# A fourth pair's token sums and 96 of 256 row pairs in seven products, in a four-layer decoder trunk

## The chip, the cores and the metric

One core of a Trainium2 chip runs the whole program. The metric is the device time of one execution in microseconds, as the median of three runs. TensorE (PE) multiplies, VectorE (DVE) and ScalarE (ACT) prepare operands and take results, SyncE (SP) and ScalarE issue the loads.

## What is computed

The reference is a trunk of two rounds over 256 tokens of width 2048, all in 32-bit floats: a mixer (round 0: a recurrent head group and pooling; round 1: sparse attention), an MLP of width 8192 and a gated embedding add. The change is in the MLPs:

```
hn = rmsnorm(h, ln_mlp_g[i])
h = h + jnp.square(jax.nn.relu(hn @ mlp_w_up[i])) @ mlp_w_down[i]
```

`mlp_w_up` is 2048 x 8192 and `mlp_w_down` 8192 x 2048.

## The kernel before

Every product of 32-bit numbers is done as three matmuls of a faster format. A weight tile `raw` is split into `hi`, its rounding (L204, ScalarE), and `lo`, the rest (L211, VectorE); the activations are split in the same way. Then `product` (L706) runs x_hi * hi (L710), x_lo * hi (L711) and x_hi * lo (L712) into one bank of PSUM. The third of them is the first that needs `lo`.

An MLP is done in 16 sets (`mm_set`): for each quarter q of the inner width two up sets, Up(q,0) and Up(q,1), and then two down sets, Down(q,0) and Down(q,1). The second number (n2) is the half of the output columns. A set gives 256 tokens x 1024 columns, from 8 pairs of rows of 128 x 2. One pair is one load of 1 MB: two rows (k) by two columns of 512 (n). With the two token halves (t) that makes a product of 2x2 by 2x2 blocks.

- A *plain* pair takes eight products, in two steps of four products (`plain`).
- An *owned* pair takes seven products (`own_fns`), in four steps of 1, 2, 2 and 2 products. For that VectorE first forms sums of the weight blocks: `first` (L735, 128x1024) and `second` (L740 and L741, 128x512 each), and the products read kept sums of the tokens, `ph["S"]`. At the end of a set `out1` to `out3` (L757 to L770) put the additional banks together.

Which pairs of a set are owned, and in what order the pairs run, stands in the constants TWO (pairs 2 and 3) and THREE (1, 2 and 3). THREE is used for Up(q,0) with q > 0 and for Down(q,1) with q < 3, TWO for all others: 38 owned pairs of 128 in an MLP, 76 of 256 in both.

```
TWO, THREE = ((2, 3), (0, 1, 4, 5, 2, 6, 3, 7)), ((1, 2, 3), (0, 4, 1, 5, 2, 6, 3, 7))
```

The token sums of the pairs 1, 2 and 3 are formed in `x_after` (`keep`, `sums`) for the MLP's input, in the sets of the mixer's out projection, and in `up_out` (`sums`, `s_back`, `s_split`) for the inner values. There each pair's sums are turned by four transposes (L963).

The order on each engine is written out by hand. `run` goes through the steps. Ahead of a step's matmuls it issues the weight sums of the step four later (SUMS) and the `hi` of the step two later (LOOK), behind them the work that `after` has put at this step, and then the `lo` of the step two later. The tile pools hold four `hi`, four `lo` and three `raw` buffers, and the weight sums use three slots. The results of a set are worked up in the first steps of the next: after a down set `adds` (L838, VectorE) and `wide` (L831), after an up set `adds` (L932), the relu and its square (ScalarE), transposes (L808) and splits (L946, L950).

The mixers' small tiles (`ttile`, 12 of 128 x 256) live in the pool `sm`, which is open for the whole program.

Of the kernel before, what the change touches and what calls it, by code (L numbers as in the profile page):

```python
# [14 lines left out]
P = 128  # L15
# [97 lines left out]
def trunk(ctx: ExitStack, tc: tile.TileContext, a: dict, out: bass.AP):  # L113
# [18 lines left out]

    def utile():
        return sm.tile([P, 4, T], F32, name="u", bufs=1)

    def ttile():
        return sm.tile([P, T], F32, name="t", bufs=12)
# [285 lines left out]
    lp = l0.enter_context(tc.tile_pool(name="lp", bufs=1))  # L423
    invc = lp.tile([P, 4, 16], F32, name="invc")
# [242 lines left out]
    def tools():  # L667

        mp = ph["mp"] = ExitStack()
        pool_ = mp.enter_context(tc.tile_pool(name="mp", bufs=1))  # L670
        m = big(F32, (P, 8, 512))
        ph["T"] = [m[:, 2 * i:2 * i + 2, :] for i in range(3)]
        ph["nT"] = 0
        ph["w2"] = m[:, 6:8, :]
        S = big()
        one = pool_.tile([P, 2, 4, T], F32R, name="s1")
        ph["S"] = []
        for i in range(2):
            two = S[:, 4 * i:4 * i + 4, :].rearrange("p a n -> p (a n)").rearrange("p (i s n) -> p i s n", i=2, s=4)
            ph["S"].append({1: one[:, i], 2: two[:, 0], 3: two[:, 1], (2, 3): two, (1,): one[:, i:i + 1]})  # L680
        ph["pT"] = pool_.tile([P, 2, 512], F32R, name="pT")
# [137 lines left out]
    TWO, THREE = ((2, 3), (0, 1, 4, 5, 2, 6, 3, 7)), ((1, 2, 3), (0, 4, 1, 5, 2, 6, 3, 7))  # L819
# [34 lines left out]
    def x_after(n2, banks, X, gi, sx=None, at=0):  # L854
# [22 lines left out]
        def keep(which):  # L877
            fx = box["fx"] = box.get("fx") or wtiles()
            for x, i in enumerate(which):
                for j in range(2):  # L880
                    act.activation(fx[len(which) - 1][:, x, j * T:(j + 1) * T], scratch(banks, i)[:, j], AF.Copy,
                                   scale=gain(2 * i + j))

        def sums(which):
            fx = box["fx"][len(which) - 1][:, :len(which)].rearrange("p i (j t) -> p i j t", t=T)
            f = s_sums(len(which), *(fx[:, :, j, t * P:(t + 1) * P] for t in range(2) for j in range(2)))
            S = ph["S"][sx][which]
            act.activation(S[:, :, :, :P], f, AF.Copy)
            after(1, lambda: dve.tensor_tensor(S[:, :, :, P:], f, S[:, :, :, :P].bitcast(F32), op=OP.subtract))
# [7 lines left out]
        if sx is not None and n2 == 0:  # L897
            after(at + 1, lambda: keep((1,)))
            after(at + 2, lambda: keep((2, 3)))
            after(at + 4, lambda: sums((1,)))  # L900
            after(at + 6, lambda: sums((2, 3)))
# [19 lines left out]
    def mlp(l, X, Xn):  # L921
# [3 lines left out]
        def up_out(q, n2):  # L925
            def post(w, banks):
# [26 lines left out]
                def sums(which):  # L953
                    v = [W[t][:, len(which) - 1].rearrange("p (i j c) -> p i j c", j=2, c=P)[:, 2 - len(which):] for t in range(2)]
                    f = s_sums(len(which), v[0][:, :, 0], v[0][:, :, 1], v[1][:, :, 0], v[1][:, :, 1])
                    for x, i in enumerate(which):
                        after(1, lambda x=x, i=i: s_back(i, f[:, x]))
                        after(2, lambda i=i: s_split(i))
# [17 lines left out]
                if n2 == 0:  # L976
                    after(3, lambda: sums((1,)))
                    after(4, lambda: sums((2, 3)))
# [9 lines left out]
        for q in range(4):  # L988
            for n2 in range(2):
# [3 lines left out]
                own, order = THREE if q and n2 == 0 else TWO  # L993
                mm_set(lambda p, q=q, n2=n2: a["mlp_w_up"][l][q][n2][p], order, X, post, own, 0)
            for n2 in range(2):
                own, order = THREE if n2 and q < 3 else TWO
# [123 lines left out]
    def open1():  # L1120
        kp = l1.enter_context(tc.tile_pool(name="kp", bufs=1))
        at["kp"] = kp
# [325 lines left out]
```

## Time and profile before

| | us |
|---|---|
| median of three runs | 2294.92 (2294.54 to 2295.27) |
| the profiled run | 2295.85 |
| its span in the profile | 2293.8 |
| TensorE busy | 2269.0, 99% |
| VectorE busy | 1797.9, 78% |
| ScalarE busy | 1340.6, 58% |

The profile is of one execution. Busy times are those in which an engine has an instruction running; a matmul's record is longer than the time to the next matmul's start, since they run one into the other. The profile's names are those of the program: `big` is any of the large tiles (activations, kept sums, weight sums), `ps` a bank of PSUM.

### The profile page before, as it was taken

How to read it: one execution, taken by the hardware profiler on the slowest of the kernel's cores; microseconds unless marked ns; L12 is line 12 of the kernel's file. 1: busy time of each engine (PE TensorE's matmuls, PEld its weight loads, DVE VectorE, ACT ScalarE, POOL GpSimd, SP SyncE). 2: the span in 40 equal slices, each digit the busy share in tenths (PEclk: the TensorE clock that was granted, in tenths of full speed). 3: DMA queues.
4: the chain of work that ended last, by engine and by line, in shares of the span. 5: the costliest groups of instructions: out<-in, count | busy, mean ns of one | idle time of the engine just before them, and what ended most of it. 6: DMA issues, size and time to landing. Idle time of an engine off the chain costs nothing.

```text
span 2293.8 us, 30360 instructions
## 1 busy us (share of the span) xinstructions
PE 2269.0 (99%) x11506; PEld 1927.0 (84%) x11506; DVE 1797.9 (78%) x2475; ACT 1340.6 (58%) x1940; POOL 14.6 (1%) x42
## 2 busy tenths in 40 slices
PE   8999999999999999999999999999999999999997
PEld 8998888888888888889889988888888888888886
DVE  6786688988988987856875676688988988988865
ACT  6665565565566565665564454566566565565654
POOL 2000000000000000000000000000000000000000
PEclk9999999999999999999999999999999999999999
DMA  7645555555555555555775224555555555555553
GB/s 259 213 155 179 204 184 202 202 184 200 204 184 196 206 185 199 187 183 204 255 275 177 87 93 159 176 184 200 190 198 196 192 199 194 194 199 191 204 194 129
DMA packets 69539, 436.58 MB, mean 190 GB/s; under 512 B 9872, under 2 KB 14352, under 8 KB 18448
## 3 DMA queue, kind: packets, MB, share of 16 engines
q1 hardware_dynamic: 64832, 427.90, 54.0%
q10 hardware_dynamic: 4560, 6.74, 0.9%
q8 instruction: 90, 1.47, 0.3%
q14 instruction: 57, 0.47, 0.1%
HBM read 432.51 MB, written 2.10 MB: 189 GB/s over the span
## 4 chain that ended last, share of the span: by engine, by line
PE 97%; DVE 1%; DMA 0%; ACT 0%; issue 0%; SPq 0%; DVEq 0%; ACTq 0%
PE ps L712 25%; PE ps L710 25%; PE ps L711 25%; PE ps L295 11%; PE ps L299 3%; PE ps L808 2%; PE ps L1390 1%; PE ps L300 1%; PE ps L1180 1%; PE ps L963 0%; DVE lo L211 0%; DMA raw<-in_ab_w_in 0%; PE ps L1332 0%; PE ps L1330 0%; PE ps L1333 0%; PE ps L588 0%
## 5 line engine op out<-in xcount | busy, mean ns | idle before, releaser
L211 DVE TENSOR_TENSOR lo<-raw,hi 128x1024 fp32r<-128x1024 f32 (+1 forms) x817 | 935.9, 1158 | 159.1 <-ACT hi L204 158.4
L204 ACT ACTIVATE hi<-raw 128x1024 fp32r<-128x1024 f32 (+1 forms) x817 | 813.3, 1008 | 382.8 <-PE ps L711 300.5
L710 PE MATMUL ps<-hi,big 128*128 128x512 f32 x2436 | 954.5, 392 | 0.0
L712 PE MATMUL ps<-lo,big 128*128 128x512 f32 x2436 | 948.8, 389 | 0.0
L711 PE MATMUL ps<-hi,big 128*128 128x512 f32 x2436 | 948.1, 389 | 0.0
L712 PEld LDWEIGHTS ps<-lo,big 128*128 128x128 f32 x2436 | 457.2, 188 | 96.2 <-DVE lo L211 0.6
L711 PEld LDWEIGHTS ps<-hi,big 128*128 128x128 f32 x2436 | 457.5, 188 | 92.9
L710 PEld LDWEIGHTS ps<-hi,big 128*128 128x128 f32 x2436 | 457.4, 188 | 92.8
L204 ACT ACTIVATE hi<-big 128x1024 fp32r<-128x1024 f32 x152 | 161.4, 1062 | 253.3 <-PE ps L711 213.2
L295 PE MATMUL ps<-big,hi 128*128 128x256 f32 x1408 | 264.5, 289 | 7.7 <-ACT hi L204 7.7
L211 DVE TENSOR_TENSOR lo<-big,hi 128x1024 fp32r<-128x1024 f32 x152 | 185.8, 1222 | 90.8 <-ACT hi L204 90.8
L295 PEld LDWEIGHTS ps<-big,hi 128*128 128x128 f32 x1408 | 223.1, 193 | 9.7 <-ACT hi L204 7.7
L295 PE MATMUL ps<-big,lo 128*128 128x256 f32 x704 | 200.5, 285 | 1.0 <-DVE lo L211 0.9
L295 PEld LDWEIGHTS ps<-big,lo 128*128 128x128 f32 x704 | 135.8, 193 | 1.6 <-DVE lo L211 1.6
L299 PE MATMUL ps<-big,hi 128*128 128x512 f32 x320 | 113.6, 398 | 0.0
L735 DVE TENSOR_TENSOR big<-raw 128x1024 f32<-128x1024 f32 x76 | 92.6, 1219 | 0.4 <-DMA raw<-in_mlp_w_down 0.2
L300 PE MATMUL ps<-big,lo 128*128 128x256 f32 x320 | 89.7, 280 | 0.6 <-DVE lo L211 0.5
L299 PEld LDWEIGHTS ps<-big,hi 128*128 128x128 f32 x320 | 60.1, 188 | 14.1
L950 DVE TENSOR_TENSOR big<-ps,big 128x512 fp32r<-128x512 f32 x64 | 41.1, 684 | 36.6 <-ACT big L946 36.6
L300 PEld LDWEIGHTS ps<-big,lo 128*128 128x128 f32 x320 | 60.3, 189 | 2.0 <-DVE lo L211 1.5
L411 ACT ACTIVATE big<-ps,gains 128x256 fp32r<-128x256 f32 x80 | 31.2, 472 | 42.6 <-PE ps L808 42.6
L741 DVE TENSOR_TENSOR big<-big,raw 128x512 f32<-128x512 f32 x76 | 52.6, 692 | 2.6
(256 smaller groups left out, 1630.2 us busy)
## 6 DMA issues: line engine op xcount, KB each, us to landing
raw<-in_mlp_w_up SPq DMA_DIRECT2D x128, 1024.0 KB, 4.9
raw<-in_mlp_w_down SPq DMA_DIRECT2D x128, 1024.0 KB, 4.9
raw<-in_c_w_in SPq DMA_DIRECT2D x36, 1024.0 KB, 4.9
raw<-in_ple_w_gate SPq DMA_DIRECT2D x32, 1024.0 KB, 4.9
raw<-in_ab_w_in SPq DMA_DIRECT2D x20, 1024.0 KB, 4.9
raw<-in_ab_w_out SPq DMA_DIRECT2D x16, 1024.0 KB, 4.9
raw<-in_c_w_out SPq DMA_DIRECT2D x16, 1024.0 KB, 4.9
raw<-in_c_cmp_w_k SPq DMA_DIRECT2D x8, 1024.0 KB, 4.9
```

What stands on the lines that cost most here:

```text
L204: act.activation(halves[s]["hi"][:, k, :w], halves[s]["src"][:, k, :], AF.Copy)
L211: dve.tensor_tensor(lo[:, k, :w], src[:, k, :], halves[s]["hi"][:, k, :w].bitcast(F32), op=OP.subtract)
L295: pe.matmul(b, lhsT=wt[:, kk, cols], rhs=x[:, x0:x0 + T], start=first and n == 0 and j % 2 == 0, stop=last and n == 2, skip_group_check=True)
L299: pe.matmul(b, lhsT=hi[:, kk, cols], rhs=x, start=first, stop=False, skip_group_check=True)
L300: pe.matmul(b[:, T:], lhsT=lo[:, kk, cols], rhs=x[:, :T], start=False, stop=last, skip_group_check=True)
L710: pe.matmul(b, lhsT=x_hi, rhs=hi[:, n, :], start=r not in begun, stop=False, skip_group_check=True)
L711: pe.matmul(b, lhsT=x_lo, rhs=hi[:, n, :], start=False, stop=False, skip_group_check=True)
L712: pe.matmul(b, lhsT=x_hi, rhs=lo[:, n, :], start=False, stop=end, skip_group_check=True)
L735: dve.tensor_tensor(t, raw[:, 0::3, :], raw[:, 1:2, :].to_broadcast([P, 2, 512]), op=OP.add)
L741: dve.tensor_tensor(t[:, 1], t[:, 0], raw[:, 2], op=OP.add)
L808: pe.transpose(b[:, j, t * P:(t + 1) * P], of(t, i // 2, (2 * i + j) % 4), ident)
L950: dve.tensor_tensor(Hs[n2][:, k:k + 2, T:], scratch(banks, i), Hs[n2][:, k:k + 2, :T].bitcast(F32), op=OP.subtract)
```

## The change

Three constants say which pairs are owned and in which order. FOUR (pairs 0 to 3) is used for Up(q,0) with q > 0 and Down(q,1) with q < 3. THREE is used for all Up(q,1), where TWO stood. TWO stays for Up(0,0), for Down(q,0) and for Down(3,1). That makes 48 owned pairs an MLP, 96 of 256 in both. The order of THREE is another: the first owned pair runs one pair later, and in THREE and FOUR the pairs 2 and 3 follow one another.

For it the token sums of pair 0 are kept too: the tile `s1` doubles, `keep` copies pair 0 also, and `sums` forms the sums of 0 and 1 together where it formed those of 1 alone. To have space, `ttile` takes its tiles from a pool that lives only as long as a mixer.

```diff
     def ttile():
-        return sm.tile([P, T], F32, name="t", bufs=12)
+        return small["tp"].tile([P, T], F32, name="t", bufs=12)
...
-        one = pool_.tile([P, 2, 4, T], F32R, name="s1")
+        one = pool_.tile([P, 2, 2, 4, T], F32R, name="s1")
...
-            ph["S"].append({1: one[:, i], 2: two[:, 0], 3: two[:, 1], (2, 3): two, (1,): one[:, i:i + 1]})
+            ph["S"].append({0: one[:, i, 0], 1: one[:, i, 1], 2: two[:, 0], 3: two[:, 1], (0, 1): one[:, i], (2, 3): two})
...
-    TWO, THREE = ((2, 3), (0, 1, 4, 5, 2, 6, 3, 7)), ((1, 2, 3), (0, 4, 1, 5, 2, 6, 3, 7))
+    TWO, THREE, FOUR = (((2, 3), (0, 1, 4, 5, 2, 6, 3, 7)), ((1, 2, 3), (0, 4, 5, 1, 6, 2, 3, 7)),
+                        (range(4), (4, 0, 5, 1, 6, 2, 3, 7)))
...
-            after(at + 1, lambda: keep((1,)))
+            after(at + 1, lambda: keep((0, 1)))
             after(at + 2, lambda: keep((2, 3)))
-            after(at + 4, lambda: sums((1,)))
+            after(at + 4, lambda: sums((0, 1)))
             after(at + 6, lambda: sums((2, 3)))
...
                 if n2 == 0:
-                    after(3, lambda: sums((1,)))
+                    after(3, lambda: sums((0, 1)))
                     after(4, lambda: sums((2, 3)))
...
-                own, order = THREE if q and n2 == 0 else TWO
+                own, order = THREE if n2 else FOUR if q else TWO
...
-                own, order = THREE if n2 and q < 3 else TWO
+                own, order = FOUR if n2 and q < 3 else TWO
...
+        small["tp"] = l1.enter_context(tc.tile_pool(name="tp1", bufs=1))
```

In the changed kernel the lines lie two to five further down: `lo` is L213, `first` L738, `second` L743 and L744, `wide` L836, `adds` L843, the token sums L818, their split L974.

VectorE at the start of a set that follows a down set. Before, a set with three owned pairs, Up(q,0) or Down(q,1), from its second `lo` on (its first two pairs are 0 and 4, plain, then 1, owned):

```order
L211 TENSOR_TENSOR lo<-raw,hi 128x1024
L838 SCALAR_TENSOR_TENSOR h<-ps,rs,h 128x512 x2
L211 TENSOR_TENSOR lo<-raw,hi 128x1024 x2
L735 TENSOR_TENSOR big<-raw 128x1024
L211 TENSOR_TENSOR lo<-raw,hi 128x512
L740 TENSOR_TENSOR big<-big,raw 128x512
L741 TENSOR_TENSOR big<-big,raw 128x512
L831 SCALAR_TENSOR_TENSOR h<-u,rs,h 128x1024
L211 TENSOR_TENSOR lo<-raw,hi 128x1024
L211 TENSOR_TENSOR lo<-big,hi 128x1024 x2
L211 TENSOR_TENSOR lo<-raw,hi 128x1024
L831 SCALAR_TENSOR_TENSOR h<-big,rs,h 128x1024
```

The same place in the changed kernel, a set with four owned pairs (pair 4 plain, then 0, owned):

```order
L213 TENSOR_TENSOR lo<-raw,hi 128x1024
L738 TENSOR_TENSOR big<-raw 128x1024
L843 SCALAR_TENSOR_TENSOR h<-ps,rs,h 128x512 x2
L213 TENSOR_TENSOR lo<-raw,hi 128x512
L743 TENSOR_TENSOR big<-big,raw 128x512
L744 TENSOR_TENSOR big<-big,raw 128x512
L213 TENSOR_TENSOR lo<-raw,hi 128x1024
L213 TENSOR_TENSOR lo<-big,hi 128x1024
L836 SCALAR_TENSOR_TENSOR h<-u,rs,h 128x1024
L213 TENSOR_TENSOR lo<-big,hi 128x1024
L213 TENSOR_TENSOR lo<-raw,hi 128x1024 x2
```

The weight sums of the first owned pair have moved ahead of the second pair of `adds` and of the narrow `lo`, and the wide add stands between two `lo` of that owned pair.

VectorE at pairs 2 and 3 near the end of a set. In the changed kernel, from the sums for pair 2 to the last `lo` of pair 3:

```order
L738 TENSOR_TENSOR big<-raw 128x1024
L213 TENSOR_TENSOR lo<-raw,hi 128x512
L743 TENSOR_TENSOR big<-big,raw 128x512
L744 TENSOR_TENSOR big<-big,raw 128x512
L213 TENSOR_TENSOR lo<-raw,hi 128x1024
L213 TENSOR_TENSOR lo<-big,hi 128x1024 x2
L738 TENSOR_TENSOR big<-raw 128x1024
L213 TENSOR_TENSOR lo<-raw,hi 128x512
L743 TENSOR_TENSOR big<-big,raw 128x512
L744 TENSOR_TENSOR big<-big,raw 128x512
L213 TENSOR_TENSOR lo<-raw,hi 128x1024
L213 TENSOR_TENSOR lo<-big,hi 128x1024 x2
```

Before, the same place has the plain pair 6 between them, two `lo` more:

```order
L211 TENSOR_TENSOR lo<-big,hi 128x1024 x2
L211 TENSOR_TENSOR lo<-raw,hi 128x1024 x2
L735 TENSOR_TENSOR big<-raw 128x1024
L211 TENSOR_TENSOR lo<-raw,hi 128x512
L740 TENSOR_TENSOR big<-big,raw 128x512
```

What moved is the plain pair 6, from between the pairs 2 and 3 to ahead of pair 2.

VectorE in Up(q,1), in the middle of the work on Up(q,0), in the changed kernel, from the token sums of 0 and 1 on (L818, two groups of four), with the splits of the turned sums at L974:

```order
L818 TENSOR_TENSOR big<-u,big 128x2x128
L213 TENSOR_TENSOR lo<-raw,hi 128x1024
L738 TENSOR_TENSOR big<-raw 128x1024
L974 TENSOR_TENSOR s_2274<-ps,s_2274 128x4x128 x2
L213 TENSOR_TENSOR lo<-raw,hi 128x512
L743 TENSOR_TENSOR big<-big,raw 128x512
L744 TENSOR_TENSOR big<-big,raw 128x512
L974 TENSOR_TENSOR big<-ps,big 128x4x128 x2
L213 TENSOR_TENSOR lo<-raw,hi 128x1024
```

Before, no weight sums stood among these: the first owned pair came two steps later, and one split was fewer.

## Rows read from the trace of the kernel before

**Rows 1.** The page: busy time of the engines, and the chain that ended last
```profile
PE 2269.0 (99%) x11506; PEld 1927.0 (84%) x11506; DVE 1797.9 (78%) x2475; ACT 1340.6 (58%) x1940; POOL 14.6 (1%) x42
PE 97%; DVE 1%; DMA 0%; ACT 0%; issue 0%; SPq 0%; DVEq 0%; ACTq 0%
```
**Rows 2.** Stretches MLP 0, Down(0,1), Up(1,1): length; engines' busy; clock, DMA share, GB/s
```profile
253.40:948.00 694.60, 694.60 (x3168) 576.68 (x3167) 596.72 (x684) 416.22 (x522) 0.00 (x0) 1.00 0.57 194
386.63:428.22 41.59, 41.59 (x184) 34.35 (x183) 38.55 (x42) 23.06 (x25) 0.00 (x0) 1.00 0.59 203
469.82:515.16 45.34, 45.34 (x216) 37.79 (x214) 38.44 (x50) 28.76 (x39) 0.00 (x0) 1.00 0.54 186
```
**Rows 3.** Timeline of TensorE in Down(0,1): start, length, instruction
```profile
415.98 0.39 PE L710 MATMUL ps<-hi,big 128*128 128x512 f32 x1
...
421.42 0.39 PE L710 MATMUL ps<-hi,big 128*128 128x512 f32 x1
```
**Rows 4.** Timeline of VectorE in Down(0,1), from pair 3's sums to the end
```profile
412.36 1.22 DVE L735 TENSOR_TENSOR big<-raw 128x1024 f32<-128x1024 f32 x1
413.49 0.69 DVE L211 TENSOR_TENSOR lo<-raw,hi 128x512 fp32r<-128x512 f32 x1
414.09 0.68 DVE L740 TENSOR_TENSOR big<-big,raw 128x512 f32<-128x512 f32 x1
...
415.42 1.22 DVE L211 TENSOR_TENSOR lo<-raw,hi 128x1024 fp32r<-128x1024 f32 x1
416.56 1.22 DVE L211 TENSOR_TENSOR lo<-big,hi 128x1024 fp32r<-128x1024 f32 x1
419.14 1.23 DVE L211 TENSOR_TENSOR lo<-big,hi 128x1024 fp32r<-128x1024 f32 x1 [1.36 <-ACT hi L204]
...
422.98 1.22 DVE L211 TENSOR_TENSOR lo<-raw,hi 128x1024 fp32r<-128x1024 f32 x1
```
**Rows 5.** Timeline of VectorE at the start of Up(1,0), which begins at 428.22
```profile
428.57 1.22 DVE L211 TENSOR_TENSOR lo<-raw,hi 128x1024 fp32r<-128x1024 f32 x1
429.70 1.41 DVE L838 SCALAR_TENSOR_TENSOR h<-ps,rs,h 128x512 f32<-128x512 f32 x2
431.02 2.35 DVE L211 TENSOR_TENSOR lo<-raw,hi 128x1024 fp32r<-128x1024 f32 x2
...
436.36 1.28 DVE L831 SCALAR_TENSOR_TENSOR h<-u,rs,h 128x1024 f32<-128x1024 f32 x1
437.56 1.22 DVE L211 TENSOR_TENSOR lo<-raw,hi 128x1024 fp32r<-128x1024 f32 x1
```
**Rows 6.** Timeline of all engines in the out projection's second half: a wait of TensorE
```profile
219.80 1.23 DVE L211 TENSOR_TENSOR lo<-raw,hi 128x1024 fp32r<-128x1024 f32 x1
...
221.08 0.50 PE L712 MATMUL ps<-lo,big 128*128 128x512 f32 x1
...
221.41 0.39 PE L710 MATMUL ps<-hi,big 128*128 128x512 f32 x1
```
**Rows 7.** Timeline of VectorE in Up(1,1), which begins at 469.82: token sums
```profile
479.86 0.28 DVE L815 TENSOR_TENSOR big<-big 128x128 f32<-128x128 f32 x1
...
480.79 1.22 DVE L211 TENSOR_TENSOR lo<-raw,hi 128x1024 fp32r<-128x1024 f32 x1
481.93 0.42 DVE L815 TENSOR_TENSOR big<-big 128x256 f32<-128x256 f32 x1
...
483.39 1.22 DVE L211 TENSOR_TENSOR lo<-raw,hi 128x1024 fp32r<-128x1024 f32 x1
```
**Rows 8.** Timeline of TensorE in Up(1,1): four transposes between matmuls
```profile
482.26 0.39 PE L712 MATMUL ps<-lo,big 128*128 128x512 f32 x1
482.49 0.60 PE L963 MATMUL ps<-ident,big 128*128 128x128 f32 x4
...
483.16 0.40 PE L711 MATMUL ps<-hi,big 128*128 128x512 f32 x1
```
**Rows 9.** Timeline of ScalarE in the out projection's second half: copies of token tiles
```profile
217.23 1.59 ACT L881 ACTIVATE big<-ps,gains 128x256 f32<-128x256 f32 x4
```

## What was predicted

> **What bounds the kernel now.** I read the page first: TensorE is busy 99% of the span and the chain that ended last is 97% TensorE [rows 1]. Then the MLPs, where the change sits, by stretch: in the 694.6 us of MLP 0 TensorE is busy throughout at a granted clock of 1.00, VectorE 596.7 us, 86% [rows 2]. An average hides the sets, so I took two apart. Down(0,1), with three owned pairs, lasts 41.59 us and VectorE is busy for 38.55 of them, 93%. Up(1,1), with two owned pairs and more work after it, lasts 45.34 with VectorE busy for 38.44 [rows 2]. So the question is whether VectorE has room in the very sets that get more owned pairs.
>
> [...] What follows rests on the rows alone.
>
> TensorE's pace: 24 matmuls of 512 columns start between 415.98 and 421.42 [rows 3], 0.2267 us each. A plain pair is 24 of them, 5.44 us, in two steps of 2.72; an owned pair 21, 4.76 us, in steps of 3, 6, 6 and 6 (0.68 and three times 1.36).
>
> VectorE's pace, by starts since the records overlap by 0.08 [rows 4]: the sum of a whole load (`first`) 1.13, the two of `second` 1.33 together, a `lo` of two rows 1.14, of one row 0.60. An owned pair is 1.13 + 1.33 + 0.60 + 3 x 1.14 = 6.48 us of VectorE for 4.76 of TensorE; a plain pair 2 x 1.14 = 2.28 for 5.44. Owned pairs run VectorE into debt by 1.7 us, plain ones pay back. The lead with which a `lo` comes is bounded: at the end of a three-pair set the `lo` from 422.98 ends at 424.20 [rows 4], and its third matmul wants it at 425.50 + 0.45 = 425.95: 1.75 us ahead. Four `hi` and four `lo` buffers allow little more right after an owned pair: the `lo` at 419.14 waited 1.36 us for its `hi` [rows 4], which waited for a buffer that TensorE held.
>
> **Part by part.** *Products.* 20 more owned pairs save 3 matmuls each: 60 x 0.2267 = 13.6 us of TensorE.
>
> *Token sums of the pair 0.* After each of the 8 sets Up(q,0) four more transposes run: four of them stretch 0.45 us between the matmuls of 482.26 and 483.16 to 0.90 [rows 8], so 8 x 0.44 = 3.5 us back on TensorE. If only products and transposes counted, the change would gain 10.1.
>
> *VectorE per added owned pair*: 6.48 - 2.28 = 4.20 us more. Down(0,1) has 41.59 - 38.55 = 3.04 idle; with a fourth pair VectorE needs 38.55 + 4.20 = 42.75 where TensorE needs 41.59 - 0.68 = 40.91. The set can't be shorter than 42.75. That is the floor, with no idle VectorE left at all. There are 12 such sets (Down(q,1) for q 0 to 2, Up(q,0) for q 1 to 3, two layers).
>
> *Where a four-pair set stalls.* I follow VectorE in its new order from the set's start; it issues in order, and TensorE waits on the `lo` it needs at the third matmul of a step. The order 4, 0, 5, 1, 6, 2, 3, 7 makes pair 0 the steps 2 to 5, pair 1 the steps 8 to 11. In the trace the set at 428.22 has its second `lo` start at 428.57 [rows 5], 0.35 in; I take 0.42, as the set before ends with VectorE 0.08 later (below). The two adds of 128x512 take 1.32, a wide add 1.20 [rows 5].
> - Step 3 (second step of pair 0, wanted at 6.12 + 0.45 = 6.57): lo 1.14, `first` 1.13, adds 1.32, narrow lo 0.60, `second` 1.33, so the lo starts at 5.94 and with its record of 1.22 ends at 7.16. Late by 0.59.
> - Step 5 (wanted at 9.29): two lo 2.28 and the wide add 1.20, start 9.42, end 10.64. Late by 1.35 against the unstalled set.
> - Step 9 (pair 1, wanted at 16.77): three lo 3.42, `first`, narrow lo, `second`, wide add 4.26, start 17.10, end 18.32. Late by 1.55.
> - A wait costs more than its lateness: TensorE started 0.05 after the lo's end (221.03 to 221.08), and the next matmul 0.33 later instead of 0.23 [rows 6]; with slower ones behind it I take 0.15 to 0.2 a wait. So 1.7 by step 9.
> - Pairs 2 and 3 stand side by side, which no set of before has. Counted from a pair's start (418.02 in the rows, 15 matmuls before 421.42), its last lo ends at 2.35 (419.14 + 1.23 - 418.02), held back by the `hi` buffer as above; then `first` 1.13, narrow lo 0.60 and `second` 1.33 come before the lo of pair 3's second step, which starts at 5.33, ends at 6.55 and is wanted at 5.44 + 0.45 = 5.89. Late by 0.66, with the restart 0.85. Bounds for this unseen neighbourhood: nothing, if the earlier delay has given VectorE its time back, up to 1.36 more, if the wait for `hi` of [rows 4] comes once more.
> Sum: 40.80 + 1.7 + 0.85 = 43.35, against 41.59 before: +1.8 a set (floor +1.16). After pair 3 the lead recovers within pair 7 to the same 1.7 as before, 0.08 less. 12 x 1.8 = 21.6 us.
>
> *Up(q,1), 8 sets, two to three owned pairs.* TensorE: 0.68 less, 0.44 more. VectorE starts as before, but the owned pair 1 comes after six plain steps where eight stood, in the middle of the post of Up(q,0). The sums of pairs 0 and 1 take 1.46 (as those of 2 and 3: 481.93 to 483.39) instead of 0.93 (479.86 to 480.79) [rows 7], and one split of 0.60 is added. By starts from the set's start at 469.82: these sums begin at 10.04 [rows 7] and take to 11.50, a lo to 12.64, the other sums to 14.10, a lo to 15.24, `first` to 16.37, two splits to 17.57, the narrow lo to 18.17, `second` to 19.50, two splits to 20.70, and the lo of step 7 ends its record at 21.92. Step 6 of before began at 45.34 - 25.84 = 19.50 (the pairs 5, 2, 6, 3, 7 that followed take 3 x 5.44 + 2 x 4.76); four transposes more make it 19.94, so step 7 wants its lo at 19.94 + 0.68 + 0.45 = 21.07. Late by 0.85, with the restart 1.05. Then the neighbours 2 and 3 again, 0.85. Together -0.68 + 0.44 + 1.05 + 0.85 = +1.7; bounds 0 (both hidden) and +3. 8 x 1.7 = 13.6 us. ScalarE has room there (28.76 of 45.34 [rows 2]).
>
> *Out projections, second halves (2 sets).* There the `lo` at 219.80 already came last, and TensorE waited for it [rows 6]; ahead of it ScalarE copies tiles one after the other [rows 9], and two more copies of 256 columns at (1.59 - 0.5) / 3 = 0.36 each push it by 0.71: 2 x 0.7 = 1.4 us.
>
> *Costs nothing*: ScalarE and VectorE each split 512 columns less per owned pair (already in the 6.48). The loads are the same megabytes in the same number, so SP's queue gets no new wait, and 0.57 of the DMA time is busy [rows 2]. The small tiles' new pools only change addresses: they open before their first writer and close long after their last reader has run; if a late reader did hold the region, the sums' first copies would wait, well under 1 us, twice.
>
> **Sum.** +21.6 + 13.6 + 1.4 = +36.6. Against the profiled execution's span of 2293.8 that is 2330; the profiled run took 2295.85, 0.9 over the median of 2294.92. On the median: **2331 us**, 1.6% slower.
>
> **Rivals.**
> (a) *Faster: the lead carries over.* Over a whole MLP VectorE would need 596.7 + 10 x 4.2 + 4 x 1.1 = 643 us in 690, and the average has room. If buffers let VectorE enter a four-pair set 2.6 us further ahead than the 1.75 of [rows 4], no wait is left, TensorE sets the time and 2294.9 - 13.6 + 3.5 = 2285 results. Against it: the lead at the end of each set is capped by buffers that this change leaves alone. 7%. If waits eat just that gain, it stays within 0.2%: 3%.
> (b) *Only the floor.* VectorE works without a gap and the neighbours cost nothing: 12 x 1.16 + 8 x 0.8 + 1.4 gives 2317. [...] Against it: VectorE did idle 3.04 in such a set, for reasons of buffers that stay. 7% (2300 to 2317), half of it below my range.
> (c) *Waits beget waits.* If VectorE's 1.36 idle per owned neighbour (waiting for `hi`) remains on top of the floor, twice in a four-pair set, that set takes 42.75 + 2.72 = 45.5: 12 x 3.9 + 13.6 + 1.4 gives 2357. Against it: a stalled TensorE frees those buffers earlier relative to VectorE's queue. 6%.
> That the pairs aren't owned at all is excluded by the order, which holds 96 `first` sums where 76 stood.
>
> **Numbers.** Forecast 77%, (a) 7 and 3%, (b) 7%, (c) 6%. The range runs from 2312, which takes in most of (b), to 2342, which takes in an extra wait of 0.5 us in each of 20 sets. Faster by over 0.2% (about what a measurement here can tell from no change): 0.07; within it 0.03; slower 0.90.
>
> **What would show it.** Right: four-pair sets of 43.0 to 43.8 us with VectorE over 97% busy; TensorE's waits on `lo` in steps 3, 5 and 9 and at the second step of pair 3, some 0.6 us each; Up(q,1) at about 47.0; Down(q,0) unchanged. Wrong: four-pair sets of 40.9 with no wait on `lo` would be (a); sets near 42.75 with no wait at pair 3 would be (b); 45 or more with VectorE idle behind `hi` would be (c). A clock below 1.00 after the new waits would add a cost that I haven't counted.

## The result, and the profile after

The changed kernel takes 2331.6 us (median of 4 runs, 2331.3 to 2332.3) where the kernel before takes 2295.1 on the same chip (2294.5 to 2295.3): a ratio of 1.016, 95% interval 1.0142 to 1.0178. It is slower by 36.5 us. The profiled execution has a span of 2330.3 us, 36.5 more than before, and its granted clock is 1.00 in every stretch of it shown below.

The page of the changed kernel, busy time of the engines, the chain that ended last, and the group of the third matmuls of the products (busy, mean ns of one, idle before them and what ended it). They answer to [rows 1]:

```profile
PE 2276.2 (98%) x11478; PEld 1913.6 (82%) x11478; DVE 1888.5 (81%) x2583; ACT 1379.4 (59%) x1992; POOL 14.6 (1%) x42
...
PE 84%; DVE 10%; ACT 3%; issue 2%; DMA 1%; SPq 0%; DVEq 0%; ACTq 0%
...
L715 PE MATMUL ps<-lo,big 128*128 128x512 f32 x2336 | 915.8, 392 | 24.0 <-DVE lo L213 24.0
```

TensorE still reads 98% busy, as it read 99% before. What tells is the chain: VectorE has gone from 1% of it to 10%, and the last row names who is late for whom: the matmul that needs `lo` was idle for 24.0 us, all of it ended by `lo`. The records of the matmuls that waited are longer (0.50 us in the rows below, where 0.39 is usual), so idle time by this row is less than what the waits cost.

Stretches of the changed kernel: MLP 0, Down(0,1), Up(1,1), Down(0,0), Up(0,1). Columns as in [rows 2], which these answer to:

```profile
253.69:966.08 712.39, 698.45 (x3153) 570.38 (x3152) 641.07 (x738) 434.40 (x546) 0.00 (x0) 1.00 0.55 189
389.11:432.45 43.34, 41.99 (x182) 33.49 (x180) 42.54 (x47) 24.67 (x27) 0.00 (x0) 1.00 0.57 195
475.78:522.82 47.04, 45.71 (x217) 37.52 (x215) 43.56 (x56) 30.87 (x42) 0.00 (x0) 1.00 0.53 180
345.16:389.11 43.95, 43.95 (x204) 36.57 (x202) 34.52 (x39) 27.67 (x36) 0.00 (x0) 1.00 0.55 191
297.63:345.16 47.53, 45.73 (x216) 37.52 (x215) 44.03 (x57) 31.00 (x42) 0.00 (x0) 1.00 0.52 178
```

MLP 0 has grown from 694.60 to 712.39. Down(0,1) went from 41.59 to 43.34 with VectorE busy for 42.54 of it, Up(1,1) from 45.34 to 47.04. Down(0,0), which keeps two owned pairs, is as it was: 43.95, measured from the first matmul of the set to that of the next.

TensorE in Down(0,1) of the changed kernel (start, length, instruction, idle before and its releaser), around the steps 3 and 5 and at pair 3:

```profile
395.45 0.39 PE L714 MATMUL ps<-hi,big 128*128 128x512 f32 x1
396.24 0.50 PE L715 MATMUL ps<-lo,big 128*128 128x512 f32 x1 [0.40 <-DVE lo L213]
396.58 0.39 PE L713 MATMUL ps<-hi,s 128*128 128x512 f32 x1
...
398.91 0.39 PE L714 MATMUL ps<-hi,s 128*128 128x512 f32 x1
399.71 0.50 PE L715 MATMUL ps<-lo,s 128*128 128x512 f32 x1 [0.41 <-DVE lo L213]
...
422.31 0.39 PE L714 MATMUL ps<-hi,big 128*128 128x512 f32 x1
423.24 0.50 PE L715 MATMUL ps<-lo,big 128*128 128x512 f32 x1 [0.54 <-DVE lo L213]
```

Such a wait is read by starts: 395.45 to 396.24 is 0.79 where 0.2267 is due, so 0.56; the next start comes 0.34 later instead of 0.23, the restart. Step 5 waits 0.57, pair 3 0.70.

VectorE there, from the last `lo` of pair 2 to the second `lo` of pair 3; it answers to [rows 4]:

```profile
417.76 1.22 DVE L213 TENSOR_TENSOR lo<-big,hi 128x1024 fp32r<-128x1024 f32 x1 [0.56 <-ACT hi L206]
418.90 1.22 DVE L738 TENSOR_TENSOR big<-raw 128x1024 f32<-128x1024 f32 x1
...
421.97 1.22 DVE L213 TENSOR_TENSOR lo<-raw,hi 128x1024 fp32r<-128x1024 f32 x1
```

The wait of `lo` for `hi`, 1.36 before, is 0.56 here, and then five instructions run without a gap until 423.19, 0.05 before TensorE's matmul of 423.24 starts.

TensorE in Up(1,1) of the changed kernel, at step 7 and at pair 3:

```profile
496.58 0.39 PE L714 MATMUL ps<-hi,big 128*128 128x512 f32 x1
497.76 0.50 PE L715 MATMUL ps<-lo,big 128*128 128x512 f32 x1 [0.79 <-DVE lo L213]
...
513.62 0.50 PE L715 MATMUL ps<-lo,big 128*128 128x512 f32 x1 [0.54 <-DVE lo L213]
```

And in the second half of the out projection, all engines; it answers to [rows 6]:

```profile
220.09 1.22 DVE L213 TENSOR_TENSOR lo<-raw,hi 128x1024 fp32r<-128x1024 f32 x1
...
221.37 0.50 PE L715 MATMUL ps<-lo,big 128*128 128x512 f32 x1 [0.53 <-DVE lo L213]
```

The account by sets, each from first matmul to first matmul: twelve four-pair sets at +1.74 (43.33 on average) are 20.9, six Up(q,1) at +1.71 and the two Up(0,1) at +2.18 are 14.6, and the two halves of the out projections at +0.73 (45.47 to 46.20) are 1.5. Together 37.0; the span grew by 36.5, the stretch ahead of the first of these halves being 0.4 shorter.

### The profile page after: what moved, and what is told of

Its sections match the earlier page's. It is cut to its first block, busy times and chain, and to the rows that moved or that the text cites. A ratio compares the mean times of both kernels' runs of the same rounds, so it can differ in the third digit from the quotient of the medians.

```text
span 2330.3 us, 30541 instructions
## 1 busy us (share of the span) xinstructions
PE 2276.2 (98%) x11478; PEld 1913.6 (82%) x11478; DVE 1888.5 (81%) x2583; ACT 1379.4 (59%) x1992; POOL 14.6 (1%) x42
## 4 chain that ended last, share of the span: by engine, by line
PE 84%; DVE 10%; ACT 3%; issue 2%; DMA 1%; SPq 0%; DVEq 0%; ACTq 0%
PE ps L715 22%; PE ps L714 21%; PE ps L713 21%; PE ps L297 10%; DVE lo L213 5%; PE ps L301 3%; PE ps L1396 1%; PE ps L302 1%; PE ps L811 1%; PE ps L1186 1%; DVE big L818 1%; ACT hi L206 1%; DVE big L955 1%; DMA raw<-in_ab_w_in 1%; DVE big L974 0%
## 5 line engine op out<-in xcount | busy, mean ns | idle before, releaser
L213 DVE TENSOR_TENSOR lo<-raw,hi 128x1024 fp32r<-128x1024 f32 (+1 forms) x817 | 925.4, 1145 | 157.1 <-ACT hi L206 156.5
L206 ACT ACTIVATE hi<-raw 128x1024 fp32r<-128x1024 f32 (+1 forms) x817 | 805.0, 997 | 360.5 <-PE ps L714 273.2
L715 PE MATMUL ps<-lo,big 128*128 128x512 f32 x2336 | 915.8, 392 | 24.0 <-DVE lo L213 24.0
L713 PE MATMUL ps<-hi,big 128*128 128x512 f32 x2336 | 915.8, 392 | 0.0
L714 PE MATMUL ps<-hi,big 128*128 128x512 f32 x2336 | 909.5, 389 | 0.0
L715 PEld LDWEIGHTS ps<-lo,big 128*128 128x128 f32 x2336 | 438.4, 188 | 134.8 <-DVE lo L213 45.2
L714 PEld LDWEIGHTS ps<-hi,big 128*128 128x128 f32 x2336 | 438.8, 188 | 89.3
L713 PEld LDWEIGHTS ps<-hi,big 128*128 128x128 f32 x2336 | 438.8, 188 | 88.5 <-ACT hi L206 0.4
L206 ACT ACTIVATE hi<-big 128x1024 fp32r<-128x1024 f32 x192 | 203.8, 1062 | 268.8 <-PE ps L714 194.2
L213 DVE TENSOR_TENSOR lo<-big,hi 128x1024 fp32r<-128x1024 f32 x192 | 231.0, 1220 | 58.1 <-ACT hi L206 58.1
L738 DVE TENSOR_TENSOR big<-raw 128x1024 f32<-128x1024 f32 x96 | 117.0, 1219 | 0.0
L955 DVE TENSOR_TENSOR big<-ps,big 128x512 fp32r<-128x512 f32 x64 | 41.2, 686 | 36.5 <-ACT big L951 36.5
L744 DVE TENSOR_TENSOR big<-big,raw 128x512 f32<-128x512 f32 x96 | 66.4, 692 | 3.3
L743 DVE TENSOR_TENSOR big<-big,raw 128x512 f32<-128x512 f32 x96 | 65.8, 686 | 0.0
```

Of the source, the lines that this page charges most:

```text
L206: act.activation(halves[s]["hi"][:, k, :w], halves[s]["src"][:, k, :], AF.Copy)
L213: dve.tensor_tensor(lo[:, k, :w], src[:, k, :], halves[s]["hi"][:, k, :w].bitcast(F32), op=OP.subtract)
L713: pe.matmul(b, lhsT=x_hi, rhs=hi[:, n, :], start=r not in begun, stop=False, skip_group_check=True)
L714: pe.matmul(b, lhsT=x_lo, rhs=hi[:, n, :], start=False, stop=False, skip_group_check=True)
L715: pe.matmul(b, lhsT=x_hi, rhs=lo[:, n, :], start=False, stop=end, skip_group_check=True)
L738: dve.tensor_tensor(t, raw[:, 0::3, :], raw[:, 1:2, :].to_broadcast([P, 2, 512]), op=OP.add)
```

## Experiments: the parts by themselves

**Token sums alone.** The sums of pair 0 are formed, turned and kept, and the small tiles have their new pools; which pairs are owned and their order are those of before.

```diff
-    THREE = ((1, 2, 3), (0, 4, 5, 1, 6, 2, 3, 7))
+    THREE = ((1, 2, 3), (0, 4, 1, 5, 2, 6, 3, 7))
...
-                own, order = THREE if n2 else FOUR if q else TWO
+                own, order = THREE if q and n2 == 0 else TWO
...
-                own, order = FOUR if n2 and q < 3 else TWO
+                own, order = THREE if n2 and q < 3 else TWO
```

> Keeps the token sums of pair 0 and the new pools, but owns the same pairs in the same order as before (TWO and THREE in their old places). My theory (VectorE delivers lo late in the sets that got one more owned pair) leaves only the price of the sums: 8 x 0.44 us of transposes and 2 x 0.73 us in the out projections, 2295 + 5 = 2300 us, Up(q,1) at 45.8. Rival: the sums and the pools, not the owned pairs, carry the loss; then well over 2310.

Measured: 2299.64 us, a ratio of 1.0020 (1.0011 to 1.0030). Down(0,1) and Up(1,1):

```profile
387.22:428.81 41.59, 41.59 (x184) 34.36 (x183) 38.53 (x42) 23.06 (x25) 0.00 (x0) 1.00 0.59 202
470.40:516.14 45.74, 45.74 (x220) 38.22 (x218) 39.49 (x51) 29.26 (x40) 0.00 (x0) 1.00 0.55 184
```

The four transposes cost 0.40 a set Up(q,1), 3.2 in eight; 1.5 in the out projections makes 4.7, and 4.7 came (against 2294.95 for the kernel before on the same chip). The new pools cost nothing that shows.

**Four-pair sets alone.** Up(q,1) goes back to two owned pairs.

```diff
-                own, order = THREE if n2 else FOUR if q else TWO
+                own, order = TWO if n2 else FOUR if q else TWO
```

> The changed kernel with two owned pairs in Up(q,1) as before; the four-pair sets stay. Theory: 12 sets of 43.34 against 41.59 on top of the price of the sums, 2300 + 21 = 2321 us. Rival (only VectorE's sum of work counts, not its order): 42.75 a set, 2300 + 14 = 2314.

Measured: 2320.24 us, 1.0110 (1.0095 to 1.0125).

**Three pairs in Up(q,1) alone.** Where before had three owned pairs, their number and order of before; Up(q,1) as changed.

```diff
+    OLD = ((1, 2, 3), (0, 4, 1, 5, 2, 6, 3, 7))
...
-                own, order = THREE if n2 else FOUR if q else TWO
+                own, order = THREE if n2 else OLD if q else TWO
...
-                own, order = FOUR if n2 and q < 3 else TWO
+                own, order = OLD if n2 and q < 3 else TWO
```

> The changed kernel without four-pair sets: three owned pairs in the old order where the kernel before has them, and the new three-pair order in Up(q,1). Theory: 8 sets of 47.05 to 47.5 against 45.34, and 1.5 us in the out projections, 2295 + 15 + 1 = 2311 us. If the waits of a set are its own, this and the four-pair run together, less the sums alone, give the changed kernel's 2332; if lateness is carried from one kind of set into the other, they fall short by several us.

Measured: 2311.48 us, 1.0072 (1.0057 to 1.0087). Down(0,1) with four pairs alone (first row), and Up(1,1) with three pairs in Up(q,1) alone (second row, from the other kernel):

```profile
386.75:430.07 43.32, 41.95 (x181) 33.49 (x180) 42.53 (x47) 24.68 (x27) 0.00 (x0) 1.00 0.57 194
```

```profile
471.90:518.94 47.04, 45.71 (x216) 37.51 (x215) 43.55 (x56) 30.86 (x42) 0.00 (x0) 1.00 0.52 179
```

The set lengths are those of the whole change, and the parts add: 2320.24 + 2311.48 - 2299.64 = 2332.1, against 2331.6 measured. So the sets don't help or hurt one another: each meets its own waits, and neither part of the change is a gain.

## Experiments: floor or local debt?

Is VectorE short of time over a whole set (42.5 us of work), or does it come late at certain places though the set has room? Four kernels take away VectorE's work or its limits.

**The wide adds left out.** In the MLPs' down sets the two `wide` of 128x1024 that stand in the next set are not done, so the additional banks don't reach `h`.

```diff
-                after(4, lambda: wide(0))
-                after(8, lambda: wide(1))
```

> The changed kernel with the wide adds of the MLPs' down sets left out (two of 128x1024 after each set with kept bank sums; the residual is not complete). That takes 2.4 us of VectorE from each four-pair set. Theory: what counts is what stands ahead of a wanted lo. The lo of step 3 has no wide add ahead of it and stays late by 0.6, those of steps 5 and 9 come in time, the neighbours stay late: 42.45 a set, 2332 - 11 = 2321 us. Rival (sum of VectorE's work): the whole 2.4 comes off until TensorE sets the time, 40.95 to 41.2 a set, 2303 to 2306.

Measured: 2322.15 us, 1.0118 (1.0101 to 1.0135). Down(0,1) as a stretch, then from timelines of VectorE and TensorE at the pairs 2 and 3:

```profile
388.74:431.26 42.52, 41.58 (x182) 33.65 (x180) 40.24 (x45) 24.66 (x27) 0.00 (x0) 1.00 0.57 198
```

```profile
416.57 1.22 DVE L213 TENSOR_TENSOR lo<-big,hi 128x1024 fp32r<-128x1024 f32 x1 [1.48 <-ACT hi L206]
...
422.05 0.50 PE L715 MATMUL ps<-lo,big 128*128 128x512 f32 x1 [0.54 <-DVE lo L213]
```

VectorE has 2.30 us less to do and the set is only 0.82 shorter. 40.24 of VectorE's work is less than the 40.80 of TensorE, and still TensorE waits: at step 3, ahead of which no wide add stands, and at pair 3 for as long as with the wide adds. There one sees where the time won went: VectorE was 0.92 further ahead and then waited 1.48 for `hi` instead of 0.56. The lead is cut off by the buffers just ahead of the place where it is needed. So the floor isn't needed to make a set late: what VectorE owes at certain places holds it at 42.5 by itself. In the changed kernel the floor lies almost there too (VectorE busy for 42.54), and the set is 0.8 over both.

VectorE's occupancy isn't enough to tell TensorE's waits here: busy for 95% of this stretch, VectorE made TensorE wait for 1.7 us and itself waited for 2.0.

**A fifth `hi` and `lo` buffer in the MLPs.** Each fifth tile comes from a pool of its own.

```diff
+    def spare(key, pool, name):
+        if ph.get("deep"):
+            ph["n" + key] = ph.get("n" + key, 0) + 1
+            if ph["n" + key] % 5 == 0:
+                pool = ph[key]
+        return pool.tile([P, 2, 512], F32R, name=name)
...
-        halves[s]["hi"] = hip.tile([P, 2, 512], F32R, name="hi")
+        halves[s]["hi"] = spare("hx", hip, "hi")
...
-        lo = halves[s]["lo"] = lop.tile([P, 2, 512], F32R, name="lo")
+        lo = halves[s]["lo"] = spare("lx", lop, "lo")
...
+        ph["hx"], ph["lx"] = (mp.enter_context(tc.tile_pool(name=n, bufs=1)) for n in ("hx", "lx"))
+        ph["deep"] = True
...
```

> The changed kernel with a fifth hi and a fifth lo buffer in the MLPs, orders as they are. Theory: the last lo of pair 2 no longer waits for a buffer, so the neighbours 2 and 3 cost nothing; the waits at steps 3, 5 and 9 stay: four-pair sets 42.5 to 42.75, Up(q,1) 46.2, 2332 - 8 - 7 = 2317 us. Rival: VectorE has no idle time to give there; 2332.

Measured: 2323.05 us, 1.0122 (1.0107 to 1.0137). Stretches Down(0,0) and Down(0,1), then VectorE (the last two `lo` of pair 2) and TensorE at pair 3's second step:

```profile
344.20:388.45 44.25, 44.25 (x204) 36.56 (x202) 34.42 (x39) 28.34 (x37) 0.00 (x0) 1.00 0.55 191
388.45:431.15 42.70, 41.98 (x181) 33.47 (x180) 42.43 (x47) 24.32 (x27) 0.00 (x0) 1.00 0.57 197
```

```profile
415.24 2.35 DVE L220 TENSOR_TENSOR lo<-big,hi 128x1024 fp32r<-128x1024 f32 x2
...
421.91 0.44 PE L724 MATMUL ps<-lo,big 128*128 128x512 f32 x1
```

The wait of `lo` for `hi` is gone and with it the one of TensorE at pair 3 (421.68 to 421.91). The set comes to 42.70 with VectorE busy for 42.43: with one more buffer it is at the floor. So what the changed kernel pays above the floor hangs on the buffers: without the wait for one of them VectorE has almost no idle time left. The gap of 0.70 at pair 3, the same in every four-pair set of the changed kernel (0.70 to 0.71), is down to 0.06 here with one buffer more: the second start behind 421.68 is that of 422.19, 0.51 later where 0.45 is due.

In time the kernel missed its expectation by 6 us, and the first row shows where: Down(0,0), which had no wait, grew from 43.95 to 44.25. TensorE in Down(1,0), from the start of its fourth step to that of its fifth:

```profile
530.23 0.40 PE L722 MATMUL ps<-hi,big 128*128 128x512 f32 x1
...
533.02 0.39 PE L722 MATMUL ps<-hi,big 128*128 128x512 f32 x1
```

Twelve matmuls take 2.79 instead of 2.72, and so do those of each fifth step (3, 8, 13 and 18 of this set), which are the ones that read the added buffers; the others keep 0.2267. In the twelve sets with two owned pairs that is 3.5 us; the eight Up(q,1), six at 46.4 to 46.5 and the two Up(0,1) at 46.8 and 46.9 where 46.2 was expected, make another 2.8. The section on the hardware comes back to it.

**Five buffers, and `hi` and `lo` issued one step further ahead.**

```diff
-            ahead = s + min(s, LOOK - 1)
+            look = 4 if ph.get("deep") else LOOK
+            ahead = s + min(s, look - 1)
```

> As the run with five buffers, and hi and lo issued three steps ahead in the MLPs where it is two. Theory: VectorE reaches the lo of steps 3 and 5 ahead of the adds and the wide add, so the lead covers most of the waits; four-pair sets near VectorE's own 42.2 to 42.75, Up(q,1) about 45.5, 2305 to 2313 us, not under 2300 as VectorE's work in a four-pair set is over TensorE's. Rival: lead doesn't carry over and the place in the queue doesn't matter; 2317 as with buffers alone.

Measured: 2321.65 us, 1.0116 (1.0101 to 1.0131): a miss, 9 to 17 us over what I expected. Stretches Down(0,0), Down(0,1) and Up(1,0):

```profile
342.48:387.37 44.89, 44.69 (x203) 36.52 (x202) 36.02 (x41) 27.83 (x36) 0.00 (x0) 1.00 0.54 189
387.37:429.02 41.65, 41.65 (x181) 33.55 (x180) 41.19 (x45) 23.41 (x27) 0.00 (x0) 1.00 0.58 200
429.02:472.09 43.07, 42.13 (x182) 33.48 (x180) 42.61 (x47) 22.88 (x26) 0.00 (x0) 1.00 0.56 196
```

Down(0,1) with four owned pairs is now 41.65, since VectorE did 1.24 us of its work in the set ahead. But the four-pair set behind it has nobody to borrow from and stays at 43.07, and Down(0,0) pays 0.94 (0.30 of it as with five buffers alone). VectorE, TensorE and ScalarE at the start of Down(1,0), in timelines of this kernel:

```profile
519.12 0.69 DVE L947 TENSOR_TENSOR u<-ps,u 128x512 f32<-128x512 f32 x1
...
521.50 0.61 ACT L953 ACTIVATE big<-big 128x512 f32<-128x512 f32 x1
...
522.17 0.33 PE L821 MATMUL ps<-ident,big 128*128 128x128 f32 x1 [0.19 <-ACT big L953]
```

The set starts at 518.77 and the result of the set ahead is worked up from 519.12 on, 0.35 into the set; in the changed kernel this begins 0.98 ahead of the set's start (521.84 against 522.82). The `lo` that was drawn forward stands in its way, and the transposes of the relu's squares, which TensorE has in its own order, wait 0.62 more. Eight Down(q,0) and six Up(q,1) make 8.7 us. So a lead can be borrowed, but what VectorE does earlier pushes other work of VectorE back, and TensorE waits for that too.

**The wide adds on GpSimd.** ScalarE scales, GpSimd adds.

```diff
+                elif X is None:
+                    act.activation(w[t], w[t], AF.Copy, scale=r[:, t:t + 1])
+                    nc.gpsimd.tensor_tensor(ht, ht, w[t], op=OP.add)
                 else:
                     dve.scalar_tensor_tensor(ht, w[t], r[:, t:t + 1], ht, op0=OP.mult, op1=OP.add)
```

> The changed kernel with the wide adds of the MLPs' down sets done by ScalarE (times the row factor) and GpSimd (add). If GpSimd's adds leave VectorE alone: 2321 us as without them. Rival: GpSimd and VectorE hinder one another while both read two tiles; then VectorE's lo is longer in those stretches and up to all of the 11 us is lost, 2321 to 2335.

Measured: 2355.94 us, 1.0265 (1.0249 to 1.0280). It is worse than either expectation: the sets are 45.36. Down(0,1) as a stretch, then GpSimd and VectorE in it:

```profile
388.18:433.54 45.36, 42.12 (x182) 33.50 (x180) 44.55 (x45) 26.51 (x29) 6.36 (x2) 1.00 0.55 185
```

```profile
396.42 3.38 POOL L837 TENSOR_TENSOR h<-h,u 128x1024 f32<-128x1024 f32 x1 [351.25 <-DVE lo L213]
...
397.44 4.57 DVE L213 TENSOR_TENSOR lo<-raw,hi 128x1024 fp32r<-128x1024 f32 x2
...
401.28 2.99 POOL L837 TENSOR_TENSOR h<-h,big 128x1024 f32<-128x1024 f32 x1 [1.49 <-ACT big L836]
...
401.94 3.41 DVE L738 TENSOR_TENSOR big<-raw 128x1024 f32<-128x1024 f32 x1
```

Two `lo`, 2.35 at other times, take 4.57, and a `first` of 1.22 takes 3.41: VectorE loses 2.2 us to each add of GpSimd, to be spared 1.2. The first add begins at 396.42 under a `lo` that started at 396.31 and runs to 397.52, and 2.28 later, at 399.80, it ends; that is, within 0.1, the time by which the two `lo` from 397.44 on are longer (2.22). What holds VectorE up in that time no run shows.

## Experiments: the order

**The order of before in Up(q,1).** Three owned pairs there, in the order 0, 4, 1, 5, 2, 6, 3, 7, so that 2 and 3 aren't neighbours and pair 1 comes one pair earlier.

```diff
-    THREE = ((1, 2, 3), (0, 4, 5, 1, 6, 2, 3, 7))
+    THREE = ((1, 2, 3), (0, 4, 1, 5, 2, 6, 3, 7))
```

In this kernel the token sums of 2 and 3 take the slot in which the weight sum of pair 1 lies, before its `hi` and `lo` are taken from it, so that pair 1 in Up(q,1) is computed from those; the instructions are the same in number and size, but two engines wait for one another there in a way of this kernel alone.

> The changed kernel with the old order 0, 4, 1, 5, 2, 6, 3, 7 of the three-pair sets, so that pairs 2 and 3 are apart in Up(q,1), and pair 1 comes two steps earlier, while VectorE still works up Up(q,0). Theory: its lo of the steps 5, 6 and 7 come late one after the other, some 4 us in all for 1.9 now; Up(q,1) at about 49.1, 2332 + 16 = 2348 us. Rival: the neighbours 2 and 3 are the main thing; without them Up(q,1) is 46.2 and the kernel 2325.

Measured: 2359.35 us, 1.0280 (1.0265 to 1.0295). TensorE in Up(1,1):

```profile
493.78 1.90 PE L968 MATMUL ps<-ident,big 128*128 128x128 f32 x8 [0.64 <-DVE big L818]
...
499.60 0.51 PE L713 MATMUL ps<-hi,s 128*128 128x512 f32 x1 [2.36 <-DVE big L974]
```

That is 11 us over what I expected, and the waits are of another kind: the first product that starts in an additional bank waits for VectorE to read the turned token sums out of banks (L974). The set takes 49.60. For the price of neighbours it says nothing. That it is worse fits the one-pair shift of the new order, which keeps pair 1 behind the token sums, but as this kernel computes with overwritten sums it doesn't show what the shift is worth.

**Four owned pairs with none side by side**, 0, 4, 1, 5, 2, 6, 3, 7, to try the neighbours where no token sums are.

```diff
-                        (range(4), (4, 0, 5, 1, 6, 2, 3, 7)))
+                        (range(4), (0, 4, 1, 5, 2, 6, 3, 7)))
```

> The changed kernel with another order of the sets with four owned pairs: 0, 4, 1, 5, 2, 6, 3, 7 instead of 4, 0, 5, 1, 6, 2, 3, 7, so that no two owned pairs stand side by side and the set begins with an owned one. Same work, same VectorE busy time (42.5 us a set). Theory: the wait of 0.83 us at pair 3 is the price of the neighbours 2 and 3 and goes; the waits at the front stay about as large (1.7 us, now in the first steps of pair 0), and the set is bounded by VectorE's 42.5: sets of 42.6 to 42.9 instead of 43.33, 12 x 0.45 to 0.75 less, 2322 to 2327 us. Rival: VectorE's debt at the start of the set is what decides; an owned pair at the very front falls onto the adds and the additional banks of the set before, the wait only moves: 43.3 or more, 2331 to 2340.

Measured: 2353.91 us, 1.0255 (1.0239 to 1.0270). TensorE in Down(0,1) at pair 3's second step, then at the start of Up(1,0); in between VectorE's adds for that set's banks:

```profile
424.63 0.39 PE L714 MATMUL ps<-hi,big 128*128 128x512 f32 x1
424.85 0.39 PE L715 MATMUL ps<-lo,big 128*128 128x512 f32 x1
...
433.69 0.39 PE L715 MATMUL ps<-lo,big 128*128 128x512 f32 x1
435.77 0.47 PE L713 MATMUL ps<-hi,big 128*128 128x512 f32 x1 [1.69 <-DVE h L843]
```

```profile
434.88 1.40 DVE L843 SCALAR_TENSOR_TENSOR h<-ps,rs,h 128x512 f32<-128x512 f32 x2
```

The stretch Up(1,0), from its first matmul to that of the next set:

```profile
435.77:479.06 43.29, 41.84 (x180) 33.63 (x181) 40.80 (x44) 23.30 (x26) 0.00 (x0) 1.00 0.56 193
```

Of my theory one part holds: pair 3 no longer waits (424.63 to 424.85 is the plain pitch), so the wait there comes of the neighbours. The rest falls, and the rival holds: the set is no shorter for it. The waits moved to the front (0.48 and 0.95 in pair 0, another 0.48 at pair 1's last step), which leaves Up(1,0) at 43.29 with VectorE busy for only 40.80 of it. What the neighbours cost a set can't be read from this order. And there is a new wait. An owned pair uses additional banks, which are the plain banks of the set ahead, and those come free only by that set's adds. With an owned pair in front TensorE waits 1.85 us for them, twelve times: 22.2, and the kernel is 22.3 slower than the changed one. So the plain pair 4 in front covers the adds.

## Why the prediction was right

*The pace.* The floor per four-pair set, 42.75 for VectorE, was 42.54 in the trace, and TensorE's own need is 40.80: both as worked out, within 0.2.

*The stalls of a four-pair set.* Late by 0.59 at step 3: 0.56 measured. Late by 1.35 in all at step 5: the steps 3 to 5 took 1.44 more than their pace, with the restarts (0.11 to 0.12 of each shows in the next start, where 0.15 to 0.2 was taken). 1.7 by step 9: 1.71. The neighbours 0.85: 0.83. A set of 43.35: 43.33. The twelve sets come to 20.9 where 21.6 was forecast, mostly because +1.76 had been rounded up to +1.8. Step by step this went the way it was followed, because VectorE's order there is fixed and each of its instructions takes the same time in every set (the 96 `first` 1.21 to 1.23 us, the 192 `lo` of weight sums too).

*Up(q,1).* The `lo` of step 7 ended its record at 21.92 after the set's start, as worked out. The step took 1.09 more than its pace (1.05 predicted), pair 3 0.82 (0.85). The four transposes were 0.40 instead of 0.44. In all +1.71 against +1.7 in six of the eight. **The term that was too small**: the two Up(0,1), each the second set of an MLP, grew by 2.18. VectorE is busy there for 44.03 instead of 43.56 (last of the stretches above); the 0.47 of further small work in that set (three instructions for the row factor `rs` of the norm, ahead of the first adds), which before was covered, now delays a late `lo`. I had priced all eight by one of the six. That is 1.0 us.

*Out projections.* 2 x 0.7: 2 x 0.73, with the wait in the same place. The `lo` starts at 220.09 instead of 219.80, in a set that begins 0.43 earlier (207.49 instead of 207.92), so it comes 0.72 later; 0.71 was worked out.

*At nothing.* Down(q,0) is unchanged, and a wait of the sums' first copies for the new pools shows in no set.

*The sum.* That 2331 meets 2331.6 so closely is in part luck: the four-pair sets were 0.7 too dear, Up(q,1) 1.0 too cheap, and the stretch ahead of the first out projection's second half, 0.4 shorter, had no term.

*The rivals.* (a), a lead that carries over, is excluded for this kernel by the four-pair sets. The experiment with five buffers and a longer reach shows what it would have taken, and that even then one set of two gets it, at the price of another. (b), only the floor, is what five buffers give (42.70); with four the wait at pair 3 stands on top. With the wide adds away, the floor lies below TensorE's need, and waits of 1.7 us stay: the rival's mechanism alone doesn't give the set's time. (c) would need VectorE's 1.36 for `hi` to stay on top; it fell to 0.56. That wait is long when VectorE is far ahead (1.48 without the wide adds) and short when it is late, so it isn't a fixed cost on top of the floor. What is left of it does stand ahead of pair 3: with five buffers it is gone, and TensorE's wait at pair 3 with it.

*The clock.* The changed kernel's waits, 0.5 to 1.4 us each, left it at 1.00 in every set of the MLPs. In another kernel it was 0.50 for 2.8 us after a wait of 2.35, as shown below.

## What to carry to other kernels

When a change trades TensorE's work for VectorE's, follow the feeding engine instruction by instruction through the new order in one stretch, by starts, and compare each result with the time at which it is wanted: that gave every wait of the sets followed here to within 0.1 us, where occupancy gave only a floor; in the two sets that weren't followed a wait was 0.5 longer. Count how far the feeder can get ahead (the buffers), because time that it wins earlier is lost again where the buffers end (without the wide adds VectorE was 0.92 further ahead, and its wait for `hi` grew from 0.56 to 1.48). And before moving heavy work to the front of a stage, see which buffers or banks it needs, and who frees them (an owned pair in front waited 1.85 us a set for banks).

## What the runs showed of the hardware that I had not expected

**VectorE's instructions were longer while GpSimd added.** Each 128x1024 add of GpSimd took 2.2 us from VectorE (two `lo` 4.57 instead of 2.35, a `first` 3.41 instead of 1.22), 1.7 times what VectorE needs for the same sum with its scaling (1.28).

**The granted clock was 0.50 for 2.8 us after a wait.** In the kernel with the order of before in Up(q,1), TensorE in Up(2,1) stood idle for 2.35 us ahead of the matmul of 679.80, for VectorE (L974), and came back at a granted clock of 0.50. Two stretches from there on:

```profile
679.80:682.60 2.80, 2.80 (x7) 2.22 (x8) 2.80 (x4) 1.40 (x3) 0.00 (x0) 0.50 0.17 70
682.60:700.00 17.40, 17.40 (x78) 14.44 (x77) 15.25 (x17) 8.68 (x10) 0.00 (x0) 0.99 0.58 188
```

At the granted clock of 0.50 matmuls start 0.43 apart, and 2.8 us later it is back. The set took 50.93, at a mean granted clock of 0.97. Up(1,1), the set shown in the experiment, had the same wait (2.36) in the same place, kept 1.00 and took 49.60. What makes the one set differ from the other stays open.

**Matmuls that read the added buffers were 3% slower.** Their starts are 0.233 apart instead of 0.2267. Three kernels looked for the reason. The first two are the kernel before with nothing but places in memory changed: an unused tile ahead of the large pools, and the pool of the small tiles opened ahead of them.

```diff
+    padp = pool("padp", 1)
+    pad = padp.tile([P, 120], F32, name="pad")
+    nc.vector.memset(pad[:, :1], 0.0)
     bigp = pool("bigp", 6)
```

> The kernel before with one unused tile of 480 bytes a partition ahead of the large pools, so that every large tile, hi and lo buffer begins at a multiple of 2048 bytes instead of 1568 above one of 4096. Same instructions. With a fifth hi and lo buffer the matmuls of each fifth step were 0.233 us apart, those of the other steps 0.2267; the added buffers stood at 4000 above a multiple of 4096. [...] Theory B (it was the distance or the pool, not the place): the pitch stays and the time is 2295.

```diff
+    sm = pool("sm", 2)
     bigp = pool("bigp", 6)
...
-    sm = pool("sm", 2)
```

> The kernel before with the pool of the small tiles opened ahead of the large ones, so that every large tile, hi and lo buffer begins at 4000 above a multiple of 4096 bytes, as the fifth buffers did. Same instructions. Theory A (the place on which a buffer begins sets the pitch): all matmuls of 512 columns go at 0.233 instead of 0.2267, some 9000 of them in the row groups: 50 to 70 us more, 2345 to 2365. Theory B (not the place): 2295.

Measured: 2294.57 us, 0.9997 (0.9988 to 1.0007), and 2293.87, 0.9993 (0.9984 to 1.0003): no change clear of noise, and the products of plain pairs keep 0.2267. So that pitch was the same with all large tiles 1568 bytes above a multiple of 4096, at multiples of 2048, and 4000 above one of 4096. But for some products a move of pools changed it, from 0.233 to 0.2267. In the kernel before, the products on the token sums of pair 1 (`s`, in a pool that is opened with the MLP, as the added buffers are) were slower too; TensorE there, the starts of two such matmuls, six apart:

```profile
399.58 0.39 PE L710 MATMUL ps<-hi,s 128*128 128x512 f32 x1
...
400.98 0.39 PE L710 MATMUL ps<-hi,s 128*128 128x512 f32 x1
```

Six take 1.40, or 0.233 each. With the pool of the small tiles opened first the same six take 1.36 (398.72 to 400.08), and Down(0,1) with its three owned pairs is 41.48 where it was 41.59 [rows 2]:

```profile
385.80:427.28 41.48, 41.48 (x184) 34.36 (x183) 38.54 (x42) 23.02 (x25) 0.00 (x0) 1.00 0.61 204
```

In twelve such sets that is 1.3 us, about what that kernel's median lies below the one of the kernel before on the same chip (2295.35). With the unused tile instead the sets stay at 41.59. Whether opening that pool first would also cure the added buffers wasn't tried. The third kernel is the kernel with five buffers, the added ones moved away from the end of the memory.

```diff
+        ph["hx"], ph["lx"] = (mp.enter_context(tc.tile_pool(name=n, bufs=1)) for n in ("hx", "lx"))
         pool_ = mp.enter_context(tc.tile_pool(name="mp", bufs=1))
...
-        ph["hx"], ph["lx"] = (mp.enter_context(tc.tile_pool(name=n, bufs=1)) for n in ("hx", "lx"))
```

> The kernel with a fifth hi and lo buffer in the MLPs (2323 us), with those two buffers opened ahead of the MLP's other tiles: they stand at 200608 and 204704 instead of 221088 and 225184 bytes. Same instructions. With them at the end of the memory the twelve matmuls of every fifth step started 0.233 us apart instead of 0.2267, 0.30 us a set of Down(q,0). Theory A (the far end of the memory): the pitch is 0.2267 throughout, Down(q,0) 43.95, in all 2317. Theory B (the buffers being apart from the other four, wherever they are): nothing changes, Down(q,0) 44.25 and 2323.

Measured: 2323.33 us, 1.0125 (1.0108 to 1.0142), with Down(0,0) at 44.25 as before the move. So the far end isn't it either; the new places lie as far above a multiple of 4096 bytes as the old ones (4000). What makes these matmuls slower stays open.
